# A two-layer decoder trunk in split fp32: chain steps of the token mixers grouped, at least 3.5 planner units apart

## The chip, the cores and the metric

The kernel runs on one core of one Trainium2 chip. The metric is the device time of one execution in microseconds, as the median of several runs. Besides, one execution is recorded by the hardware profiler; its trace is what the text reads.

## The reference

256 tokens of width 1024 go through two layers. Each layer is a half-step SwiGLU FFN, a token mixer, and another half-step FFN. Beside the mixer's own heads stand four heads that attend to 256 memory rows; both share one input projection and one output projection. Cut to what matters:

```python
mem_kv = rms_norm(mem, mem_norm_g) @ mem_w_kv            # keys and values of the memory heads
for i in range(2):
    x = x + 0.5 * swiglu(rms_norm(x, ffn1_norm_g[i]), ffn1_w_in[i], ffn1_w_out[i])
    hn = rms_norm(x, mix_norm_g[i])
    if i == 0:                                           # mixer A
        proj = hn @ a_w_in[0]
        y_tok = mlstm_heads(...)                         # 4 heads: decay-weighted scores, numerators, per-head norm, gate
        w_out = a_w_out[0]
    else:                                                # mixer B
        proj = hn @ b_w_in[0]
        y_tok = swa_heads(...)                           # 16 query heads, 2 key heads, window 128, sinks, QK norm, rotary
        w_out = b_w_out[0]
    y_mem = memory_heads(...)                            # QK norm, softmax over 256 rows
    x = x + concatenate([y_tok, y_mem]) @ w_out
    x = x + 0.5 * swiglu(rms_norm(x, ffn2_norm_g[i]), ffn2_w_in[i], ffn2_w_out[i])
```

## The kernel before

**Projections.** All big products are computed in three matmuls: weights and activations are split into a high part rounded to fp32r and the remainder (`split`, L211 on ScalarE for the high part, L212 on VectorE for the low part), and `mm3` (L225 to L227) multiplies high by high, high by low and low by high into one PSUM bank. A weight tile is 128x1024 and feeds 24 such matmuls. Five raw tiles and eight split pairs rotate, so loading and splitting run ahead of TensorE. This sequence of projection matmuls is called the stream here.

**Chains.** What the mixers compute between the projections are chains of small dependent steps. A step has some TensorE instructions (fp32 matmuls, or transposes through the identity, L236), and then work on VectorE, ScalarE and GpSimd whose result the chain's next step needs on TensorE. In mixer B:
- keys: one turn (`turn`, four 128x128 transposes into one bank), a scaled copy;
- each of four query groups: `head_norm` (square on ScalarE, sum L374, scale L377, a power on GpSimd L379, scale L381, product L383, which is the last reader of the group's PSUM bank), rotary embedding (L857 to L860), then a turn and a scaled copy, which spawns two `head` chains;
- `head`, for a pair of query heads: mask and scores into two banks (L920, L925), maxima (L929, L930), minima with the sink (L932, L933), exponentials (L132 is the line of every ScalarE activation), sum, reciprocal, scaling (L946); then six transposes and copies (L954); then the value product (L961) and its split (L245, L246);
- each of the two memory query groups: `head_norm`, a turn, and two memory heads: scores against `kT` (L231), maxima L591, exponentials, scaling L596; four transposes and a copy (L603); a product with `vM` (L231) and its split (L245, L246).

Mixer A has the same memory heads, and for its own four heads gate columns, scores, numerators and a turn.

**The order.** TensorE's and SyncE's instructions are issued in exactly the order in which the program emits them. The other engines' order is set by a scheduler that knows the data dependences. A planner, `Weave`, fixes TensorE's order: `run` walks the main generator (the stream), which yields after every 12 matmuls or so. `now` is the planner's own clock: every emitted matmul adds its assumed cost (0.328 for the three of `mm3`, 0.107 for a transpose). A chain yields the spacing after which its next step is due (table `LAT`, in the same units, about microseconds). After each yield of the stream all due chain steps are emitted; since a step itself moves `now`, further steps can become due in the same loop. `need` makes the stream wait for a chain's result; then the earliest step is emitted at once.

**PSUM.** There is one pool of eight banks (`mo`). Every group of projections, turn, score or product takes one; a head pair's scores take two. A new user waits for the last reader of the bank that it is given.

Of the kernel before, what the change touches and what calls it, by code (L numbers as in the profile page):

```python
# [32 lines left out]
def constants():  # L33
# [16 lines left out]

LAT = dict(pieces=1, norm=7.5, norm_b=4.8, mnorm=2.4, x0=16.0, x0_b=7.5, mkeys=7.2, cross=9.5, cross_s=1.5,
           cross_m=3.7, cross_p=8.7, cross_o=3.0, gates=20.0, scores=2.2, scores_m=8.4, num=6.9, num_r=7.5,
           keys=5.5, keys_d=7.2, query=9.0, head=1.5, head_m=2.5, head_p=9.3, head_o=4.0)


WARM = 18
# [2 lines left out]
class Weave:  # L61
# [5 lines left out]

    def __init__(self):
        self.now, self.live, self.seq = 0.0, [], 0

    def spawn(self, chain, delay=0.0):
        self.live.append([self.now + delay, self.seq, chain])
        self.seq += 1
# [12 lines left out]
    def run(self, main):  # L86
        for need in main:
            while need is not None and not need():
                self.step(min(self.live, key=lambda c: (c[0], c[1])))
            c = self.ready()  # L90
            while c is not None:
                self.step(c)
                c = self.ready()
        while self.live:
            self.step(min(self.live, key=lambda c: (c[0], c[1])))

# [2 lines left out]
def tile_trunk(ctx: ExitStack, tc: tile.TileContext, a, out):  # L99
# [11 lines left out]
    wv = Weave()  # L111
# [24 lines left out]
    def table(name):  # L136

        with tc.issue_after(tabled[0].ins):
            nc.scalar.preload_act_table_set(name)

    def unit(dt):
        return mk(up, [P, 2, T], dt, "u")

    def tmp():
        return mk(tp, [P, 2, T], F32, "t")
# [4 lines left out]
    def mo():  # L150
        return mk(pb8, [P, 512], F32, "bank")

    def halves(ps):
        return ps.rearrange("p (h t) -> p h t", h=2)
# [48 lines left out]
    pieces = [1]  # L203
# [12 lines left out]
    def wtile(src, nk, ncol=256):  # L216
        raw = mk(wrp, [P, nk, ncol], F32, "wr")
        nc.sync.dma_start(raw, src)
        return split(raw, [P, nk, ncol])
# [4 lines left out]
    def mm3(ps, wh, wl, xh, xl, start, stop):  # L224
        nc.tensor.matmul(ps, wh, xh, start=start, stop=False, skip_group_check=True)  # L225
        nc.tensor.matmul(ps, wh, xl, start=False, stop=False, skip_group_check=True)  # L226
        nc.tensor.matmul(ps, wl, xh, start=False, stop=stop, skip_group_check=True)  # L227
        wv.now += 0.328
# [28 lines left out]
    def pair(x):  # L257
        return x.unsqueeze(1).to_broadcast([P, 2, T])


    class Norm:
# [30 lines left out]

        def chain(self, gap=LAT['norm_b']):
            pc = mo()
            for h in range(2):
                mmf(pc[:, h:h + 1], self.acc[:, 0, h * P:(h + 1) * P], ones, 1)
            self.rc = mk(sp, [P, 2], F32, "rc")
            rsqrt_cols(self.rc, pc[:, 0:2], 2, 1.0 / D)
            if not self.rows:
                self.done = True  # L300
                return
            yield gap
            ps = mo()
            bcast_rows(ps, self.rc)
            self.rb = mk(sp, [P, T], F32, "rb")
            nc.scalar.copy(self.rb, ps[:, :T])
            if self.half:
                self.hrb = mk(sp, [P, T], F32, "hrb")
                act(self.hrb, ps[:, :T], AF.Copy, scale=0.5)
            self.done = True  # L310
# [57 lines left out]
    def head_norm(dst, src, n, hsc):  # L368

        hd = src.shape[2] // n  # L370
        sq, v, u = tmp(), col(), col()
        sqv = sq[:, :, :n * hd]
        act(sqv, src, AF.Square)
        nc.vector.tensor_reduce(out=v[:, 0:2 * n].rearrange("p (h m) -> p h m", h=2),  # L374
                                in_=sqv.rearrange("p h (m d) -> p h m d", m=n), axis=AX.X, op=ALU.add)
        for h in range(2):
            nc.vector.tensor_scalar(u[:, n * h:n * h + n], v[:, n * h:n * h + n], hsc[:, h:h + 1], EPS,  # L377
                                    op0=ALU.mult, op1=ALU.add)
        nc.gpsimd.tensor_tensor(out=u[:, 8:8 + 2 * n], in0=u[:, 0:2 * n], in1=mhalf[:, 0:2 * n], op=ALU.pow)  # L379
        for h in range(2):  # L380
            nc.vector.tensor_scalar(v[:, 8 + n * h:8 + n * h + n], u[:, 8 + n * h:8 + n * h + n],  # L381
                                    hsc[:, 2 + h:3 + h], None, op0=ALU.mult)
        tt(out=dst.rearrange("p h (m d) -> p h m d", m=n), in0=src.rearrange("p h (m d) -> p h m d", m=n),  # L383
           in1=v[:, 8:8 + 2 * n].rearrange("p (h m) -> p h m", h=2).unsqueeze(3).to_broadcast([P, 2, n, hd]),
           op=ALU.mult)
# [12 lines left out]
    x0 = Norm(G_F1)  # L398

    def memory():  # L400
# [22 lines left out]
        def keys(gi, kr):  # L423
            nc.scalar.copy(kT[gi], turn(kr))
            return
            yield

        for gi in range(2):
# [13 lines left out]
            norm.fold()  # L442
            wv.spawn(norm.chain(), LAT['mnorm'])
            gv = Group(wkv, 512, mh, ml, rows=True)
# [5 lines left out]
            for i, q in enumerate((first, gr)):  # L450
                kr = tmp()
                head_norm(kr, q.ps, 2, hsc)
                wv.spawn(keys(i, kr), LAT['mkeys'] + 1.5 * i)
        for gi in range(2):
# [7 lines left out]
            if gi == 0:  # L462
                with tc.issue_after(last[0].ins):
                    for c2 in range(4):
                        x0.put(xT[c2])
                wv.spawn(x0.chain(LAT['x0_b']), LAT['x0'])

# [41 lines left out]
    def ffn(x, w_in, w_out, nxt=None, mid=None):  # L509

        pieces[0] = 1
        hh, hl = [], []
        yield from ffn_in(x, w_in, hh, hl, mid)
        w = w_out.rearrange("(k p) f -> p k f", p=P)

        def products(ps, m, kg, wt, start):
            ms = slice(m * P, (m + 1) * P)
            for k in range(kg[1]):
                kc = kg[0] + k
                mm3(ps, wt[0][:, k, ms], wt[1][:, k, ms], hh[kc // 2][:, kc % 2], hl[kc // 2][:, kc % 2],  # L520
                    start=kc == 0 and start, stop=kc == 21)

        for c2 in range(4):
            wts = [(kg, w[:, kg[0]:kg[0] + kg[1], c2 * 256:(c2 + 1) * 256]) for kg in KG]
            if nxt is None and c2 == 3:
                wts = [(kg, wtile(src, kg[1])) for kg, src in wts]
                y = tmp()
                for m in range(2):
                    ps = mo()[:, :T]
                    for kg, wt in wts:  # L530
                        products(ps, m, kg, wt, True)
                        yield
                    tt(out=y[:, m], in0=ps, in1=x.hrb, op=ALU.mult)
                    tt(out=y[:, m], in0=y[:, m], in1=x.xT[c2][:, m], op=ALU.add)
                    nc.scalar.dma_start(out[:, 2 * c2 + m], y[:, m])
                return
            ps = mo()
            for kg, src in wts:
                wt = wtile(src, kg[1])
                for m in range(2):  # L540
                    products(ps[:, m * T:(m + 1) * T], m, kg, wt, m == 0)
                    yield
            t = tmp()
            tt(out=t, in0=halves(ps), in1=pair(x.hrb), op=ALU.mult)
            xn = unit(F32)
            tt(out=xn, in0=t, in1=x.xT[c2], op=ALU.add)
            if nxt is None:
                nc.scalar.dma_start(out[:, 2 * c2:2 * c2 + 2], xn)
            else:
                nxt.put(xn)  # L550
        wv.spawn(nxt.chain(), LAT['norm'])

# [15 lines left out]
    def cross_spawn(gr, gi, layer, hsc, ys):  # L568
# [4 lines left out]
        def queries():  # L573
# [4 lines left out]
            for m in range(2):  # L578
                wv.spawn(head(m), LAT['cross_s'] + LAT['cross_m'] * m)
            return  # L580
# [68 lines left out]
    def mixer_a(x, nxt):  # L649
        w = a["a_w_in"][0]  # L650
        table("sigmoid_and_others")
        pieces[0] = LAT['pieces']
        ys = Heads()
        og, qk, sd = [], {}, {}

# [207 lines left out]
    def mixer_b(x, nxt):  # L863
        w = a["b_w_in"][0]
        pieces[0] = LAT['pieces']
        table("natural_log_exp_and_others")
        ys = Heads()
        st = {}
# [107 lines left out]
    def program():  # L976
        yield from memory()
        x1, x2, x3 = Norm(G_MIX, half=False), Norm(G_F2), Norm(G_F1 + 8)
        x4, x5 = Norm(G_MIX + 8, rows=False), Norm(G_F2 + 8)
        yield from ffn(x0, a["ffn1_w_in"][0], a["ffn1_w_out"][0], x1, late_constants)  # L980
        yield from mixer_a(x1, x2)
        yield from ffn(x2, a["ffn2_w_in"][0], a["ffn2_w_out"][0], x3)
        yield from ffn(x3, a["ffn1_w_in"][1], a["ffn1_w_out"][1], x4, rope_tables)
        yield from mixer_b(x4, x5)
        yield from ffn(x5, a["ffn2_w_in"][1], a["ffn2_w_out"][1])
# [41 lines left out]
```

## Time and profile before

| | |
|---|---|
| median of three runs | 1012.15 us (1011.66 to 1013.83) |
| the profiled execution | 1012.23 us, span 1010.4 us |
| busy: TensorE, VectorE, ScalarE, GpSimd | 998.5, 655.5, 519.5, 35.7 us |
| mixer A, from its first chain step to the next norm | 257.79 to 357.75 us |
| mixer B, between the norms before and behind it | 719.40 to 833.89 us |

Times inside the trace count from the span's start. A row of the chain or of the timeline names the line of the program, the engine, the operation and the tiles written and read. TensorE's matmuls are pipelined: a row's duration contains the way through the array, so what an instruction costs is the distance from its start to the next start. A transposed or fp32 matmul is emitted once and can show as more than one instruction.

### The profile page before, as it was taken

The page shows a single profiled execution, that of the slowest core. Times are in us where ns is not written, and L with a number is a line of the kernel's source. Part 1 is how long each engine was busy: PE and PEld are TensorE (multiplying, and loading weights), DVE is VectorE, ACT ScalarE, POOL GpSimd, SP SyncE. Part 2 cuts the span into 40 slices and gives each one's busy share as a digit, 9 for nine tenths or more (in the row PEclk, how much of TensorE's full clock was granted, in tenths as well). Part 3 has the DMA queues.
Part 4 walks back from the last instruction along what each step waited for, and adds up shares of the span by engine and source line. Part 5 has one row for each costly group of instructions (what it writes and reads, how often), then busy time and mean ns, then how long its engine had stood idle before and what let it go on. Part 6 is the DMA issues. An engine that isn't in the chain of part 4 may idle for free.

```text
span 1010.4 us, 20624 instructions
## 1 busy us (share of the span) xinstructions
PE 998.5 (99%) x8594; PEld 980.2 (97%) x8594; DVE 655.5 (65%) x1063; ACT 519.5 (51%) x764; POOL 35.7 (4%) x32
## 2 busy tenths in 40 slices
PE   8999999999999999999999999999999999999998
PEld 7999999999999999999999999999987899999998
DVE  6866665577856676665558666656787766666551
ACT  7754445446656554444445544544557754454440
POOL 1200000000001000000000000000121000000000
PEclk9999999999999999999999999999999999999999
DMA  9776656666644566665676666567541347666550
GB/s 308 242 245 200 192 180 185 199 183 179 184 139 133 167 210 195 200 189 170 192 206 205 189 191 201 173 197 198 182 131 66 100 131 220 198 189 185 188 170 21
DMA packets 173204, 182.70 MB, mean 181 GB/s; under 512 B 7124, under 2 KB 168328, under 8 KB 173112
## 3 DMA queue, kind: packets, MB, share of 16 engines
q1 hardware_dynamic: 171872, 179.60, 58.3%
q10 hardware_dynamic: 1016, 1.58, 0.5%
q8 instruction: 67, 1.10, 0.5%
q0 software_dynamic: 224, 0.22, 0.2%
q14 instruction: 25, 0.20, 0.1%
HBM read 180.32 MB, written 1.05 MB: 180 GB/s over the span
## 4 chain that ended last, share of the span: by engine, by line
PE 94%; DVE 3%; ACT 1%; DMA 1%; POOL 0%; issue 0%; SPq 0%; ACTq 0%
PE bank L225 30%; PE bank L226 30%; PE bank L227 30%; PE bank L231 2%; PE bank L236 1%; ACT u L132 1%; DVE wl L212 1%; DMA wr<-in_mem_w_kv_dram 1%; PE bank L961 1%; POOL col L379 0%; DVE col L930 0%; DVE u L383 0%; DVE col L591 0%; PE bank L925 0%; DVE u L946 0%
## 5 line engine op out<-in xcount | busy, mean ns | idle before, releaser
L212 DVE TENSOR_TENSOR wl<-wr,wh 128x1024 fp32r<-128x1024 f32 (+1 forms) x347 | 414.7, 1196 | 279.8 <-ACT wh L211 279.0
L211 ACT CAST wh<-wr 128x1024 fp32r<-128x1024 f32 (+1 forms) x347 | 356.8, 1031 | 393.1 <-PE bank L226 368.9
L225 PE MATMUL bank<-xh,wh 128*128 128x256 f32 x1544 | 429.1, 278 | 0.0
L226 PE MATMUL bank<-xl,wh 128*128 128x256 f32 x1544 | 426.8, 276 | 0.0
L227 PE MATMUL bank<-xh,wl 128*128 128x256 f32 x1544 | 426.8, 276 | 0.0
L226 PEld LDWEIGHTS bank<-xl,wh 128*128 128x128 f32 x1544 | 290.3, 188 | 0.1
L225 PEld LDWEIGHTS bank<-xh,wh 128*128 128x128 f32 x1544 | 290.0, 188 | 0.1
L227 PEld LDWEIGHTS bank<-xh,wl 128*128 128x128 f32 x1544 | 289.9, 188 | 0.0
L225 PE MATMUL bank<-u,wh 128*128 128x256 f32 x896 | 249.3, 278 | 0.0
L226 PE MATMUL bank<-u,wh 128*128 128x256 f32 x896 | 247.6, 276 | 0.0
L227 PE MATMUL bank<-u,wl 128*128 128x256 f32 x896 | 247.6, 276 | 0.0
L225 PEld LDWEIGHTS bank<-u,wh 128*128 128x128 f32 x896 | 168.2, 188 | 1.9 <-issue 1.7
L226 PEld LDWEIGHTS bank<-u,wh 128*128 128x128 f32 x896 | 168.4, 188 | 0.1
L227 PEld LDWEIGHTS bank<-u,wl 128*128 128x128 f32 x896 | 168.3, 188 | 0.0
L225 PE MATMUL bank<-wh,xh 128*128 128x256 f32 x208 | 59.7, 287 | 0.0
L226 PE MATMUL bank<-wl,xh 128*128 128x256 f32 x208 | 57.9, 278 | 0.0
L227 PE MATMUL bank<-wh,xl 128*128 128x256 f32 x208 | 57.9, 278 | 0.0
L476 DVE TENSOR_TENSOR t<-bank,rb 128x256 f32<-128x256 f32 x88 | 36.6, 420 | 7.3 <-PE bank L227 7.3
L225 PEld LDWEIGHTS bank<-wh,xh 128*128 128x128 f32 x208 | 39.1, 188 | 0.5 <-issue 0.3
L226 PEld LDWEIGHTS bank<-wl,xh 128*128 128x128 f32 x208 | 39.1, 188 | 0.1
L227 PEld LDWEIGHTS bank<-wh,xl 128*128 128x128 f32 x208 | 39.0, 187 | 0.0
L479 DVE TENSOR_TENSOR t<-t,bank 128x256 f32<-128x256 f32 x88 | 32.7, 412 | 1.8 <-ACT t L132 1.8
(171 smaller groups left out, 657.5 us busy)
## 6 DMA issues: line engine op xcount, KB each, us to landing
wr<-in_ffn_w_in_dram SPq DMA_DIRECT2D x176, 512.0 KB, 3.6
wr<-in_ffn_w_out_dram SPq DMA_DIRECT2D x80, 512.0 KB, 3.5
wr<-in_a_w_in_dram SPq DMA_DIRECT2D x28, 512.0 KB, 3.9
wr<-in_b_w_in_dram SPq DMA_DIRECT2D x14, 512.0 KB, 4.6
wr<-in_a_w_out_dram SPq DMA_DIRECT2D x12, 512.0 KB, 3.3
wr<-in_b_w_out_dram SPq DMA_DIRECT2D x12, 512.0 KB, 3.4
wr<-in_ffn_w_out_dram SPq DMA_DIRECT2D x16, 256.0 KB, 2.8
wr<-in_mem_w_kv_dram SPq DMA_DIRECT2D x7, 512.0 KB, 8.0
```

Of the source, the lines that this page charges most:

```text
L132: ins = nc.scalar.activation(*args, **kw)
L211: last[0] = nc.scalar.copy(hi[:, i * n:(i + 1) * n], src[:, i * n:(i + 1) * n])
L212: tt(out=lo[:, i * n:(i + 1) * n], in0=src[:, i * n:(i + 1) * n], in1=hi[:, i * n:(i + 1) * n].bitcast(F32), op=ALU.subtract)
L225: nc.tensor.matmul(ps, wh, xh, start=start, stop=False, skip_group_check=True)
L226: nc.tensor.matmul(ps, wh, xl, start=False, stop=False, skip_group_check=True)
L227: nc.tensor.matmul(ps, wl, xh, start=False, stop=stop, skip_group_check=True)
L231: nc.tensor.matmul(ps, lhsT, rhs, start=start, stop=stop, skip_group_check=True)
L236: nc.tensor.transpose(ps, src, ident[:k, :k])
L476: tt(out=t[:, m], in0=ps[m][:, :T], in1=x.rb, op=ALU.mult)
L479: tt(out=t[:, m], in0=t[:, m], in1=ps[m][:, T:], op=ALU.mult)
L961: nc.tensor.matmul(o[es[e], cs], vr[:, i, js], pTs[e][:, src], start=i == 0, stop=i == 1, skip_group_check=True)
```

## The change

Three things. `Weave` gets a grain: after chain steps have been emitted, the next ones are emitted only when the planner's clock has moved on by `grain` units, and then all that are due. The mixers set it to 3.5, the FFNs to 0. And five spacings in `LAT` change: the memory heads' scores come 2.5 instead of 1.5 units behind their turn, the second head of a group 3.0 instead of 3.7 behind the first, the memory heads' value product 3.5 instead of 3.0 behind its copy; in mixer B the first pair's scores come 2.5 instead of 1.5 units behind the query turn, and the second pair's 1.0 instead of 2.5 behind the first.

```diff
-LAT = dict(pieces=1, norm=7.5, norm_b=4.8, mnorm=2.4, x0=16.0, x0_b=7.5, mkeys=7.2, cross=9.5, cross_s=1.5,
-           cross_m=3.7, cross_p=8.7, cross_o=3.0, gates=20.0, scores=2.2, scores_m=8.4, num=6.9, num_r=7.5,
-           keys=5.5, keys_d=7.2, query=9.0, head=1.5, head_m=2.5, head_p=9.3, head_o=4.0)
+LAT = dict(pieces=1, norm=7.5, norm_b=4.8, mnorm=2.4, x0=16.0, x0_b=7.5, mkeys=7.2, cross=9.5, cross_s=2.5,
+           cross_m=3.0, cross_p=8.7, cross_o=3.5, gates=20.0, scores=2.2, scores_m=8.4, num=6.9, num_r=7.5,
+           keys=5.5, keys_d=7.2, query=9.0, head=2.5, head_m=1.0, grain=3.5, head_p=9.3, head_o=4.0)
...
     def __init__(self):
         self.now, self.live, self.seq = 0.0, [], 0
+        self.grain, self.fired = 0.0, 0.0
...
         for need in main:
             while need is not None and not need():
                 self.step(min(self.live, key=lambda c: (c[0], c[1])))
-            c = self.ready()
+            c = self.ready() if self.now >= self.fired + self.grain else None
             while c is not None:
                 self.step(c)
                 c = self.ready()
+                self.fired = self.now
...
     def ffn(x, w_in, w_out, nxt=None, mid=None):
 
         pieces[0] = 1
+        wv.grain = 0.0
...
         pieces[0] = LAT['pieces']
+        wv.grain = LAT['grain']
```

The last pair of lines stands at the head of both mixers. No instruction is added or taken away; TensorE's order changes within the two mixers, and with it the order of the other engines there and the banks that are given out.

1 line of the change is left out of this document (added).

## The prediction

> **What bounds the kernel now.** I read the head of the page, then the windows by stage, then TensorE's waits in the second mixer, then the order of time there.
>
> ```profile
> span 1010.4 us, 20624 instructions
> ## 1 busy us (share of the span) xinstructions
> PE 998.5 (99%) x8594; PEld 980.2 (97%) x8594; DVE 655.5 (65%) x1063; ACT 519.5 (51%) x764; POOL 35.7 (4%) x32
> ```
>
> TensorE sets the time. The profiled execution took 1012.23 us, 1.83 us more than its span and 0.08 us over the median; my sum is made against 1012.23.
>
> ```profile
> 257.79:357.75 99.96, 99.96 (x814) 97.95 (x813) 67.85 (x131) 59.86 (x112) 3.21 (x4) 1.00 0.48 148
> 357.75:719.40 361.65, 361.65 (x3191) 361.65 (x3189) 230.88 (x318) 176.29 (x212) 2.24 (x2) 1.00 0.64 195
> 719.40:833.89 114.49, 109.16 (x894) 98.27 (x894) 84.99 (x233) 71.23 (x175) 13.82 (x8) 1.00 0.36 113
> ```
>
> The columns are stretch, length, then busy time (and instructions) of PE, PEld, DVE, ACT, POOL, then the granted clock. The first row is mixer A from its first chain step on, the second nearly all FFN, the third mixer B. Only the mixers' order changes, so only rows one and three can move. FFN matmuls follow each other every 361.65 / 3191 = 0.113 us. In mixer A TensorE never idles; in mixer B it idles 114.49 - 109.16 = 5.3 us:
>
> ```profile
> PE bank L231 <- ACT u L132: 1.5, 1, 1.5
> PE bank L925 <- ACT u L132: 1.4, 1, 1.4
> PE bank L231 <- ACT t L603: 1.1, 1, 1.1
> ```
>
> These and three shorter ones are chain steps whose operand was late. A matmul counts as busy for 0.28 us but its successor could have started 0.11 us after it, so each of the six waits costs about 0.17 to 0.28 us more than its row; from start to start I count **7.0 us of waits in mixer B now**.
>
> **What a switch from the stream to a chain step costs.** This is what setting steps together could save.
>
> ```profile
> 729.38 0.60 PE L236 MATMUL bank<-con,u 128*128 128x128 f32 x4
> 729.74 0.37 PE L225 MATMUL bank<-wh,xh 128*128 128x256 f32 x1
> 729.94 0.28 PE L226 MATMUL bank<-wl,xh 128*128 128x256 f32 x1
> ...
> 732.65 0.27 PE L236 MATMUL bank<-con,u 128*128 128x128 f32 x1
> ```
>
> Four transposes alone hold TensorE for 0.36 us, and the first stream matmul behind them takes 0.20 instead of 0.12. So the return costs 0.09 us. Between 729.94 and 732.65 lie 23 matmuls, one every 0.118 us: after a switch the stream runs either at 0.118 or at the FFN's 0.113, and about half of the mixers' stretches show the slow one.
>
> ```profile
> 746.27 1.04 PE L236 MATMUL bank<-con,u 128*128 128x128 f32 x8
> 747.15 1.03 PE L231 MATMUL bank<-kT,u 128*128 128x256 f32 x4
> 747.82 0.47 PE L225 MATMUL bank<-wh,xh 128*128 128x256 f32 x1
> ```
>
> Joined, two turns take 0.88 us, 0.44 each, where one alone with its return takes 0.36 + 0.09 = 0.45. A score step of a memory head takes 0.67 here. So a step set behind another pays nearly the return it saves; joining is worth 0 to 0.1 us each.
>
> **The sum, mixer A.** In the built order of the changed kernel the 17 places where chain steps interrupt mixer A's stream become 13. The links of every chain lie 36 or more stream matmuls apart (36 x 0.113 = 4.1 us), no step is brought close behind its producer, and the present trace shows no wait there. Joining saves up to 0.2 us. The cadence of 696 matmuls can turn out all fast or all slow; that is -1.3 to +1.7 us, and I take -0.2, the half and half of now.
>
> **The sum, mixer B.** 22 interruptions become 11; I take 11 x 0.1 = 1.1 us off. But the order does more than space the steps. Every step moves the planner's clock on, which makes further steps due, and the inner loop takes them all before it looks at the grain again. At the fourth interruption after the first (144 matmuls on) one bunch holds six turns (T), six of the eight head pairs' scores (H), the four value products of the memory heads and two pairs' six transposes, with no projection between. Unhindered its length is:
>
> ```profile
> 784.56 0.50 PE L920 MATMUL bank<-maskb,identb 128*128 128x384 bf16 x2
> 784.99 0.93 PE L925 MATMUL bank<-u,u 64*128 64x128 f32 x8
> 785.85 0.39 PE L225 MATMUL bank<-u,wh 128*128 128x256 f32 x1
> ```
>
> H is 785.85 - 784.56 = 1.29 us; 6 x 1.29 + 6 x 0.44 + 4 x 0.67 (value products as the score step) + 2 x 0.66 (six transposes as 6/8 of 0.88) = 14.4 us. It starts at about 751.0: 729.38, plus four stretches of 36 with their return (4.3 to 4.4 each), plus steps of 0.36, 0.36, 1.1 and 2.5 us.
>
> Does what it needs exist by then? The first limit is the vector queue, which is worked off strictly in order.
>
> ```profile
> 736.10 0.68 DVE L374 TENSOR_REDUCE col<-t 128x8 f32<-128x512 f32 x1
> 736.82 0.36 DVE L377 TENSOR_SCALAR col<-col,qsc 128x4 f32<-128x4 f32 x2
> 737.09 1.22 DVE L212 TENSOR_TENSOR wl<-wr,wh 128x1024 fp32r<-128x1024 f32 x1
> 739.84 0.36 DVE L381 TENSOR_SCALAR col<-col,qsc 128x4 f32<-128x4 f32 x2 [1.53 <-POOL col L379]
> 740.11 0.68 DVE L591 TENSOR_REDUCE col<-bank 128x2 f32<-128x512 f32 x1
> 740.71 0.68 DVE L383 TENSOR_TENSOR u<-bank,col 128x512 f32<-128x512 f32 x1
> ```
>
> ```profile
> L212 DVE TENSOR_TENSOR wl<-wr,wh 128x1024 fp32r<-128x1024 f32 x26 | 31.5, 1220 | 10.6 <-ACT wh L211 10.6
> ...
> L383 DVE TENSOR_TENSOR u<-bank,col 128x512 f32<-128x512 f32 x6 | 4.1, 688 | 0.3
> ...
> L596 DVE TENSOR_TENSOR u<-u,col 128x512 f32<-128x512 f32 x4 | 2.7, 687 | 0.1
> L591 DVE TENSOR_REDUCE col<-bank 128x2 f32<-128x512 f32 x4 | 2.7, 681 | 0.0
> ```
>
> ```profile
> L379 POOL TENSOR_TENSOR col<-col,mhalf 128x8 f32<-128x8 f32 x4 | 8.3, 2073 | 38.6 <-DVE col L377 38.6
> ```
>
> A query group's norm is L374, L377, a power on POOL, L381, L383. Up to the first group's L374 the queues stand as before, so 736.10 holds. From there to the third group's L383 the changed vector order has five weight subtractions (6.1), three L374 and three L383 (4.1), maxima and scalings of four memory heads (4 x 0.681 + 4 x 0.687 = 5.5), and small ones: twelve L377/L381 at 0.18 (2.2), two ropes (estimated 2), reciprocals (0.6). That is 20.5 us, less 2.5 because a successor starts some 0.07 us before its forerunner's end. In two of the three norms L381 now stands right behind L377, where L212 stood between: the queue idles a whole power (2.07 each), in the third most of it is covered (0.9 left). Waits for exponentials add an estimated 1.3. So the third L383 ends at 736.1 + 20.5 - 2.5 + 5.0 + 1.3 = 760.4. TensorE wants the PSUM bank which it frees for the bunch's fourth turn, at 751.0 + 3 x 0.44 + 2 x 1.29 = 754.9, and loses **5.5 us** there or just before. At present projections stand between these parts.
>
> The second limit is ScalarE. The first pair's maxima stand behind that L383, so its exponentials begin at about 762.8.
>
> ```profile
> 756.68 0.37 ACT L132 ACTIVATE u<-bank,col 128x128 f32<-128x128 f32 x1 [2.02 <-DVE col L932]
> ...
> 758.37 0.38 ACT L132 ACTIVATE u<-bank,col 128x128 f32<-128x128 f32 x1
> ```
>
> ```profile
> L954 ACT COPY t<-bank 128x384 f32<-128x384 f32 x16 | 7.0, 493 | 1.2 <-PE bank L236 1.0
> L132 ACT ACTIVATE u<-bank,col 128x128 f32<-128x128 f32 x16 | 6.0, 376 | 10.3 <-DVE col L932 10.3
> L245 ACT CAST u<-bank 128x256 fp32r<-128x256 f32 x12 | 4.6, 386 | 4.1 <-PE bank L961 3.9
> L132 ACT ACTIVATE t<-bank 128x512 f32<-128x512 f32 x6 | 3.7, 616 | 2.3 <-PE bank L227 2.3
> ```
>
> One pair takes 758.37 - 756.68 = 1.69 us. The bunch's last scores need a bank that the fourth pair's second exponential frees: three pairs (5.1), four L245, two L954, three copies of 512 (4.4), two exponentials (0.8), with some 1.6 us of waits for maxima, so 762.8 + 11.9 = 774.7; scores then end at 775.8. The bunch lasts 24.8 instead of 14.4 us: **10.4 us of waits**. Two interruptions later the fourth group's L383 stands behind four L954 and another power; its bank and one behind it, freed by an L246 that a rope and an L212 precede, are late by an estimated 1 + 2 us. The remaining steps lie far enough apart. Waits in mixer B: 13.4 against 7.0. Sum: 1012.2 + 6.4 - 1.1 - 0.2 = **1017.3 us**. POOL's power took from 1.0 to 2.5 us in single cases, and what stands between the powers is estimated; +-3 us on the waits and the cadence give 1013.9 to 1021.5 for this case.
>
> DMA is no term: the projections' weight tiles are prefetched eight deep, and SP's order of transfers is the same.
>
> The granted clock is 1.00 in all three rows above, with waits of up to 1.5 us. [...]
>
> **The rivals.** *Faster, the vector queue in time.* Each microsecond by which the third L383 ends ahead of 760.4 takes one off. If the powers take 1.0 us and nothing waits for exponentials, and the queue's small items are half of mine, it ends near 754 (760.4 - 3.0 - 1.3 - 2.4); the bunch then ends near 769 with 3.7 us of waits, and if the fourth group's 3 us shrink to 1 likewise, mixer B has 4.7 instead of 7.0: 1012.2 - 2.3 - 1.3 = 1008.6. It decides at about 755: a later end makes the kernel slower. For it: DVE is busy only 85 of 114 us in mixer B. Against it: its idle time lies mostly at the end, where no chain is left.
>
> *No change, cadence and joining.* 1320 matmuls of the mixers run half at 0.118. If the longer stretches all came out at 0.113, that is 2.9 us off; with 3 us less of waits than I count the time is 1017.3 - 2.9 - 3 = 1011.4, and 1009 to 1014 with either alone or more. For it: stretches behind some turns return to 0.113 at once. Against it: nothing in the order selects them.
>
> [...]
>
> **How the numbers follow.** The forecast has 0.62, the vector queue in time 0.16, cadence and joining 0.18 (0.12 within 0.2%, about what a measurement of this kernel can tell, and 0.06 faster), the clock 0.04. Slower by over 0.2% (above 1014.2): 0.66; within: 0.12; faster: 0.22. The range reaches from 1008.0, which leaves out about a tenth below, to 1021.5.
>
> **What would show it.** Right: one interruption of some 25 us in mixer B, about 22 us after its first turn, with waits for L383 and for exponentials; mixer B near 120 us, mixer A within 1.5 us of 99.96, the other stretches unchanged. Wrong: a bunch under 18 us, or mixer A off by over 2 us. The joining is wrong if two turns and a score step together cost over 0.3 us less than apart.

## The result, and the profile after

| | before | after |
|---|---|---|
| median of 18 runs each | 1012.35 us (1011.66 to 1013.88) | 1015.13 us (1014.30 to 1017.24) |
| profiled execution: time, span | 1012.23, 1010.4 us | 1015.03, 1013.2 us |
| ratio after to before | | 1.0024, 95% interval 1.0017 to 1.0032 |

The changed kernel is slower. The direction was forecast, the size was not: the medians differ by 2.8 us where 5.1 were forecast. By the ratio and its interval, the loss is 0.17 to 0.32%, or 1.7 to 3.2 us.

The head of the page of the changed kernel shows the same instructions on TensorE and the same busy time; the span is 2.8 us longer.

```profile
span 1013.2 us, 20631 instructions
PE 998.6 (99%) x8594; PEld 981.3 (97%) x8594; DVE 655.2 (65%) x1063; ACT 519.3 (51%) x764; POOL 32.4 (3%) x32
```

The windows by stage, cut at the same events as before (mixer A from its first chain step, the FFNs, mixer B):

```profile
257.93:357.83 99.90, 99.90 (x815) 98.00 (x814) 67.82 (x131) 59.79 (x112) 2.79 (x4) 1.00 0.47 148
357.83:719.47 361.64, 361.64 (x3190) 361.64 (x3189) 230.89 (x318) 176.31 (x212) 2.24 (x2) 1.00 0.64 195
719.47:836.75 117.28, 110.10 (x894) 99.58 (x894) 85.08 (x233) 70.95 (x175) 12.99 (x8) 0.97 0.35 110
```

Mixer A has 99.90 us (99.96 before), the FFNs 361.64 (361.65). All of the difference lies in mixer B: 117.28 against 114.49 us. Its granted clock is 0.97, not 1.00; that comes from one place, the bunch.

The bunch in the order of time on TensorE, where the number in brackets is the idle time ahead of a row and what ended it (at the second row that is a reciprocal, L598, the last event that the trace shows there):

```profile
751.63 0.60 PE L238 MATMUL bank<-con,u 128*128 128x128 f32 x4
752.64 0.63 PE L238 MATMUL bank<-con,u 128*128 128x128 f32 x4 [0.41 <-DVE col L598]
...
756.75 0.32 PE L925 MATMUL bank<-maskb,identb 128*128 128x384 bf16 x1 [1.55 <-ACT u L134]
...
761.08 1.12 PE L238 MATMUL bank<-con,u 128*128 128x128 f32 x4 [3.16 <-DVE u L385]
761.99 1.92 PE L233 MATMUL bank<-t,vM 128*128 128x256 f32 x4
763.70 1.06 PE L238 MATMUL bank<-con,u 128*128 128x128 f32 x4
...
768.45 1.03 PE L233 MATMUL bank<-t,vM 128*128 128x256 f32 x4
769.31 0.49 PE L925 MATMUL bank<-maskb,identb 128*128 128x384 bf16 x2
...
771.70 0.48 PE L925 MATMUL bank<-maskb,identb 128*128 128x384 bf16 x2 [0.24 <-ACT t L959]
...
774.75 0.32 PE L925 MATMUL bank<-maskb,identb 128*128 128x384 bf16 x1 [0.56 <-ACT u L134]
...
775.86 0.39 PE L227 MATMUL bank<-wh,xh 128*128 128x256 f32 x1
```

It begins at 751.63 and the stream returns at 775.86: 24.23 us for one interruption. The turn at 761.08 waits for the product of the third query group's norm (L383 before, L385 here). The vector queue ahead of it:

```profile
755.68 0.67 DVE L376 TENSOR_REDUCE col<-t 128x8 f32<-128x512 f32 x1
...
756.86 0.35 DVE L379 TENSOR_SCALAR col<-col,qsc 128x4 f32<-128x4 f32 x2
757.13 1.22 DVE L214 TENSOR_TENSOR wl<-wr,wh 128x1024 fp32r<-128x1024 f32 x1
759.87 0.36 DVE L383 TENSOR_SCALAR col<-col,qsc 128x4 f32<-128x4 f32 x2 [1.53 <-POOL col L381]
760.34 0.69 DVE L385 TENSOR_TENSOR u<-bank,col 128x512 f32<-128x512 f32 x1
760.95 0.28 DVE L934 TENSOR_REDUCE col<-bank 128x1 f32<-128x128 f32 x1
```

The product ends at 761.03, and the turn starts 0.05 us later. The first pair's maxima (L934) stand right behind the product, though that pair's scores were done at about 754.4; its exponentials follow only then, on ScalarE:

```profile
762.99 0.37 ACT L134 ACTIVATE u<-bank,col 128x128 f32<-128x128 f32 x1 [5.34 <-DVE col L937]
...
764.69 0.38 ACT L134 ACTIVATE u<-bank,col 128x128 f32<-128x128 f32 x1
```

What the forecast's sum did not have is the granted clock (the third column from the end) in four windows of the bunch:

```profile
757.00:761.08 4.08, 0.92 (x9) 0.52 (x8) 2.45 (x7) 0.66 (x2) 2.54 (x1) 0.67 0.59 203
761.08:764.55 3.47, 3.47 (x12) 2.95 (x13) 3.33 (x16) 1.56 (x8) 0.00 (x0) 0.50 0.03 8
764.55:766.18 1.63, 1.63 (x12) 0.68 (x10) 1.33 (x7) 1.63 (x10) 0.00 (x0) 0.79 0.00 0
766.18:768.01 1.83, 1.83 (x11) 1.49 (x9) 1.81 (x10) 1.83 (x7) 0.00 (x0) 1.00 0.00 0
```

A mean of 0.67 over 4.08 us is half speed in its last 2.7 us; 0.79 over 1.63 us is half speed in its first 0.7. So the clock was halved from 758.4 to 765.2, 6.8 us. The product at 761.99 holds TensorE for 1.71 us (to 763.70), where one of the same shape takes 0.86 later on (768.45 to 769.31).

The next interruption, and the one after it, the fourth query group's place:

```profile
780.29 1.52 PE L966 MATMUL bank<-t,u 128*64 128x256 f32 x16
781.74 1.53 PE L238 MATMUL bank<-con,u 128*128 128x128 f32 x12
783.03 0.37 PE L227 MATMUL bank<-u,wh 128*128 128x256 f32 x1
...
787.30 1.52 PE L966 MATMUL bank<-t,u 128*64 128x256 f32 x16
788.75 0.87 PE L238 MATMUL bank<-con,u 128*128 128x128 f32 x6
790.78 0.87 PE L238 MATMUL bank<-con,u 128*128 128x128 f32 x6 [1.16 <-DVE u L248]
791.41 0.36 PE L227 MATMUL bank<-u,wh 128*128 128x256 f32 x1
```

The latter takes 4.11 us, where 28 instructions of the same kinds took 2.74 at 780.29: one wait, for L248, and none for the product L385.

### The profile page after: what moved, and what is told of

It reads as the page before. It is cut to its first block, busy times and chain, and to the rows that moved or that the text cites. A ratio compares the mean times of both kernels' runs of the same rounds, so it can differ in the third digit from the quotient of the medians.

```text
span 1013.2 us, 20631 instructions
## 1 busy us (share of the span) xinstructions
PE 998.6 (99%) x8594; PEld 981.3 (97%) x8594; DVE 655.2 (65%) x1063; ACT 519.3 (51%) x764; POOL 32.4 (3%) x32
## 3 DMA queue, kind: packets, MB, share of 16 engines
q10 hardware_dynamic: 1016, 1.58, 0.5%
## 5 line engine op out<-in xcount | busy, mean ns | idle before, releaser
L214 DVE TENSOR_TENSOR wl<-wr,wh 128x1024 fp32r<-128x1024 f32 (+1 forms) x347 | 414.6, 1196 | 288.7 <-ACT wh L213 287.7
```

The costliest lines, as they stand in the source:

```text
L214: tt(out=lo[:, i * n:(i + 1) * n], in0=src[:, i * n:(i + 1) * n], in1=hi[:, i * n:(i + 1) * n].bitcast(F32), op=ALU.subtract)
```

## The experiments

For all of them mixer B is given from the first matmul of the norm step ahead of it to that of the norm step behind it (0.36 us more than the window that starts behind the norm step; expectations may count either way). "Bunch" is its longest interruption. An FFN stretch in which the stream ran at 0.118 us throughout costs some 6.5 us more; it is told beside mixer B, since it hides what a kernel's order does. It comes and goes between executions of one kernel (e4's runs lie at 1015 to 1016 or at 1022 to 1024 us; the one in its trace, at 1015.06, has none), so the medians mix both, and mixer B in the trace is the better measure of the order. Some executions also have a low clock early on: in the traces of e10, e11 and e12 the mean over the whole execution is 0.997 or 0.998, with 1.00 in the windows from 40 to 1004 us, and mixer B begins at 720.61 to 720.66 us, against 719.04 to 719.26 before, after and in e4 and e9. Mixer B has a spread of its own: each kernel has one trace, and kernels whose order in mixer B is the same on every engine gave 118.31 and 117.49 us (e1, e4) and 115.33 and 114.53 (e10, e13 below), since more of the stream ran at 0.118 in the longer ones (474 matmuls against 281, 478 against 288). So differences under 0.8 us in that column are not told apart.

| kernel | grain | spacings | mixer B | bunch | slow FFN stretch in the trace | median, us | ratio to before |
|---|---|---|---|---|---|---|---|
| before | none | old | 114.86 | 6.98 | none | 1012.35 | 1 |
| after | both mixers | new | 117.64 | 24.23 | none | 1015.13 | 1.0024 [1.0017, 1.0032] |
| e1 | mixer A | new | 118.31 | 7.52 | last | 1022.69 | 1.0082 [1.0054, 1.0110] |
| e2 | both, only steps due at entry | new | 123.16 | 11.79 | none | 1020.23 | 1.0067 [1.0046, 1.0088] |
| e3 | none, two steps at a time | new | 123.69 | 9.92 | none | 1021.92 | 1.0082 [1.0059, 1.0105] |
| e7 | none, one step at a time | new | 121.41 | 6.06 | last | 1020.21 | 1.0070 [1.0053, 1.0086] |
| e4 | none | new | 117.49 | 7.53 | none | 1022.04 | 1.0070 [1.0044, 1.0095] |
| e8 | both mixers | old | 118.49 | 19.11 | none | 1016.90 | 1.0042 [1.0030, 1.0054] |
| e9 | none | new for memory heads | 115.97 | 7.51 | none | 1013.45 | 1.0005 [0.9994, 1.0016] |
| e10 | none | new for query heads | 115.33 | 6.98 | last | 1019.80 | 1.0081 [1.0064, 1.0099] |
| e5 | after, no power | new | 109.77 | 18.18 | first | 1013.42 | 0.9993 [0.9971, 1.0015] |
| e6 | before, no power | old | 110.25 | 6.67 | first | 1013.85 | 0.9987 [0.9963, 1.0011] |
| e11 | after, power on ScalarE | new | 109.69 | 18.14 | none | 1008.18 | 0.9960 [0.9948, 0.9972] |
| e12 | before, power on ScalarE | old | 110.37 | 6.79 | none | 1007.84 | 0.9958 [0.9945, 0.9972] |

**Is it the bunch? e1: the grain in mixer A alone.** In mixer B:

```diff
-        wv.grain = LAT['grain']
+        wv.grain = 0.0
```

> The changed kernel with the grain in mixer A alone; the new spacings stay in both mixers. Theory bunch (the loss is the waits of the one long bunch in mixer B, which only the grain builds): mixer A stays at 99.9 us, mixer B has no group of chain steps over 10 us and lies within 1.5 us of the 114.5 of before; time 1011 to 1013.5. Rival spacings (the longer spacings themselves delay the chains): mixer B stays near 117.3 and the time near 1015.

Measured: without the bunch mixer B is no shorter, 118.31 us, as the rival said. The stream is broken 22 times again, and its longest interruptions take 6.6, 7.5, 6.1 and 5.7 us. So taking away the bunch does not give back the loss: the smaller orders that the new spacings make have waits of their own.

**e2: only the steps due at entry.** The inner loop no longer takes what its own steps make due.

```diff
-            c = self.ready() if self.now >= self.fired + self.grain else None
-            while c is not None:
+            due = [c for c in self.live if c[0] <= self.now] if self.now >= self.fired + self.grain else []
+            for c in sorted(due, key=lambda c: c[1]):
                 self.step(c)
-                c = self.ready()
+            if due:
                 self.fired = self.now
```

> The changed kernel, but the inner loop emits only the steps that were due when it was entered; what becomes due while it runs waits for the next grain. Mixer B's largest group is then five turns' worth of transposes, two products and three pairs of scores instead of 112 instructions of every kind. Theory bunch: mixer B loses most of the 9.8 us of waits of the bunch and lasts 108 to 113 us, time 1006 to 1011, so faster than both. Rival grain (spacing steps 3.5 units apart delays the chains whatever the groups): 1014 to 1017.

Measured: mixer B 123.16 us, far outside both expectations. The bunch is halved and the chains end later. Here the clock halves under the stream itself:

```profile
768.79:774.45 5.66, 5.66 (x25) 5.37 (x26) 3.83 (x7) 2.94 (x5) 2.40 (x1) 0.50 0.31 97
```

24 stream matmuls take 5.66 us, 0.236 each on the mean; at a clock of 1.00 they take 0.113 or 0.118.

**e3 and e7: two steps, and one step, after each yield.** Without grain:

```diff
-            c = self.ready() if self.now >= self.fired + self.grain else None
-            while c is not None:
+            c, n = (self.ready() if self.now >= self.fired + self.grain else None), 0
+            while c is not None and n < 2:
                 self.step(c)
-                c = self.ready()
+                c, n = self.ready(), n + 1
```

> The new spacings, no grain, but at most two chain steps after each yield of the stream, in both mixers: no group of steps in mixer B holds more than a few. Theory bunch: waits in mixer B fall below the 7 us of before, mixer B 109 to 113 us, while mixer A has 19 interruptions instead of 17 and stays within 1 us of 99.96; time 1007 to 1011. Rival (few interruptions are what counts): mixer B has more interruptions than in either kernel and gets longer than 114.5, time 1013 to 1016.

> The new spacings, no grain, and one chain step at most after each yield of the stream: mixer A has 26 interruptions instead of 17 (before) and 13 (changed), none with a wait near, so mixer A alone prices an interruption. Theory (a step set behind another pays nearly the return it saves): mixer A 99.96 plus 0 to 0.1 us each, so 100 to 101, give or take 1.5 for the stream's two cadences. Rival (each interruption costs a fixed 0.3 us or more): mixer A 103 or longer. Mixer B: waits fall, but its last steps come 60 matmuls later; 109 to 114 us. Time 1007 to 1013.

Measured: mixer B 123.69 and 121.41 us, where 109 to 113 and 109 to 114 were expected: smaller groups do not take the waits away. e7 also prices the interruption as such: mixer A took 133.81 us with 27 interruptions, 133.95 with the 18 of before (the 17 of the prediction and the one behind its norm step) and 133.89 with the 14 of after, from norm to norm. Interrupting the stream costs nothing that can be seen there. (e3's mixer A, with 20, took 134.72; one wait of 0.3 us is in it.)

**e4 and e8: the spacings alone, and the grain alone.** e4 sets the grain to 0 in both mixers, e8 keeps the grain and takes back the five spacings:

```diff
-           ... head=2.5, head_m=1.0, grain=3.5, head_p=9.3, head_o=4.0)
+           ... head=2.5, head_m=1.0, grain=0.0, head_p=9.3, head_o=4.0)
```

> The new spacings without any grain (the order in mixer B is that of e1). Theory bunch: mixer B as in e1 within 0.5 us, mixer A with 17 interruptions within 1 us of 99.96, time 1011 to 1013.5. Rival spacings: mixer B near 117, time near 1015. Beside e1 it prices the grain in mixer A alone: joining worth 0.2 us there, so the two differ by less than 1 us.

> The grain of 3.5 in both mixers with the five spacings of before; it completes the square with the changed kernel (both) and the spacings alone (mixer B 117.49). Its biggest bunch is smaller by two turns, two pairs' scores and one value product than the changed kernel's. Theory 'spacings' (the five longer or shorter spacings alone put steps where operands are late, and the grain on top costs nothing): mixer B 113.5 to 115.5, as before. Theory 'bunch' (the grain's one big interruption costs by itself, and the spacings cost by another way that the grain removes): mixer B 116.5 to 119. Mixer A 133.9 from norm to norm by both.

Measured: mixer B grows by 2.6 us with the spacings alone, by 3.6 with the grain alone, and by 2.8 with both. Each part costs by itself about what both cost together, so the two costs don't add. e8's 118.49 lies in the range of its theory 'bunch', in which the two parts cost by different ways. The rows of the waits speak for one and the same limit, products of the vector queue that come late; they don't prove it, for the power was not taken out of these two kernels. In e4, in small pieces:

```profile
753.10 0.63 PE L238 MATMUL bank<-con,u 128*128 128x128 f32 x4 [0.95 <-DVE u L385]
...
783.41 0.32 PE L925 MATMUL bank<-maskb,identb 128*128 128x384 bf16 x1 [1.25 <-DVE u L385]
```

and in e8 in one piece, for one product of that line:

```profile
762.03 0.82 PE L925 MATMUL bank<-maskb,identb 128*128 128x384 bf16 x2 [3.10 <-DVE u L385]
```

In e8 the clock is halved as well, from 757.6 to 767.8 us. By the distances of the same steps at full clock the work under it is some 3.4 us longer (an estimate), so how e8's loss divides between the waits and the clock stays open. e4's clock is 1.00 all through mixer B.

**e9 and e10: the spacings in two halves.** Without grain, e9 changes the three of the memory heads, e10 the two of the query heads.

> No grain; only the three spacings of the memory heads are changed (2.5, 3.0, 3.5), the two of the query heads are those of before. TensorE's order up to the sixth interruption behind the memory scores is the same as with all five spacings. If the memory heads' spacings carry the loss of the spacings alone: mixer B 116.5 to 118. If the query heads' do: 114 to 115.

> No grain; only the two spacings of the query heads' scores are changed (2.5, 1.0), the three of the memory heads are those of before. If the memory heads' spacings carry the loss of the spacings alone: mixer B 114 to 115. If the query heads' do: 116.5 to 118.

Measured: 115.97 and 115.33 us, +1.1 and +0.5; both expected that one half would carry the loss, and neither does. The +0.5 is within the spread (e13, with the same order in mixer B, took 114.53). Together they cost 2.6, so an interplay of 1 us or more is left that no run splits further. e10 is also a warning: its mixer B is 0.5 us longer than before, its median 7.5. The window of its last FFN stretch, and that of the changed kernel:

```profile
842.30:1014.64 172.34, 172.34 (x1465) 172.34 (x1465) 93.20 (x119) 69.00 (x80) 0.00 (x0) 1.00 0.49 159
```

```profile
843.24:1009.12 165.88, 165.88 (x1466) 165.88 (x1465) 93.22 (x119) 69.08 (x80) 0.00 (x0) 1.00 0.54 165
```

The same matmuls, TensorE never idle, the clock 1.00, and 6.5 us apart.

**e5 and e6: the power taken out.** In both kernels GpSimd's power in the norm is replaced by a VectorE instruction that writes 1.0, so that the inverse root is left out of the norms of queries, keys and memory queries in both mixers:

```diff
-        nc.gpsimd.tensor_tensor(out=u[:, 8:8 + 2 * n], in0=u[:, 0:2 * n], in1=mhalf[:, 0:2 * n], op=ALU.pow)
+        nc.vector.tensor_scalar(u[:, 8:8 + 2 * n], u[:, 0:2 * n], 0.0, 1.0, op0=ALU.mult, op1=ALU.add)
```

> The changed kernel with GpSimd's power in the query and key norms replaced by a small VectorE instruction that writes 1.0 (so the inverse root is left out of these norms). The order of the projections and chain steps on TensorE is the same. Theory of the two limits (the bunch waits first for the vector queue, which idles behind the power, then for ScalarE): the L383 of the third query group ends some 5 us earlier, the bunch shrinks from 24.2 to 18.5 to 20.5 us, the 4.1 us group behind it to about 2.9; time 1009 to 1011.5. Rival (ScalarE's work alone sets the bunch): the bunch stays above 22 us, time above 1013.

> The same replacement in the kernel before. Theory: three of the six waits there follow a norm, so mixer B gains 2 to 4 us: 1008.5 to 1010.5; after e5 the change would then cost 0 to 2 us instead of 2.8. Rival (the power is covered in the finer order): under 1 us of gain, above 1011.5.

Measured: the changed kernel's bunch falls from 24.23 to 18.18 us, the fourth group's interruption from 4.11 to 2.92, mixer B to 109.77. The kernel before comes to 110.25. Both traces have a slow first FFN stretch, which hides the gain in the medians. Without the power the change costs nothing in mixer B; it is 0.5 us shorter there, which is within the spread.

**e11 and e12: the power on ScalarE.** The same with the values kept, in mixer B's norms:

```diff
-        nc.gpsimd.tensor_tensor(out=u[:, 8:8 + 2 * n], in0=u[:, 0:2 * n], in1=mhalf[:, 0:2 * n], op=ALU.pow)
+        if lnexp[0]:
+            act(u[:, 8:8 + 2 * n], u[:, 0:2 * n], AF.Ln)
+            act(u[:, 8:8 + 2 * n], u[:, 8:8 + 2 * n], AF.Exp, scale=-0.5)
+        else:
+            nc.gpsimd.tensor_tensor(out=u[:, 8:8 + 2 * n], in0=u[:, 0:2 * n], in1=mhalf[:, 0:2 * n], op=ALU.pow)
...
+        lnexp[0] = True
```

> The changed kernel, with the power on GpSimd in mixer B's norms of queries and memory queries replaced by a logarithm and an exponential of -0.5 times it on ScalarE (same values). Theory 'two limits' (the vector queue idles behind the power, then ScalarE's exponentials end the bunch): the power of 1.0 to 2.5 us becomes two small activations, some 0.5 us with their start, so the bunch falls from 24.2 to 18.5 to 21 us and mixer B from 117.3 to 110.5 to 113.5. Rival: the two activations queue on ScalarE behind weight casts of 1.2 us and copies, so nothing is won: bunch 23 to 26 us, mixer B 116.5 to 119.

> The kernel before with the same replacement as in the run of the changed kernel with logarithm and exponential on ScalarE (mixer B 109.69 there, 117.64 without it, from norm to norm). Theory 'the change costs through the vector queue behind the power': with the short norm the kernel before gains less, since its finer order hid more of the power; mixer B 109.5 to 111.5 (from 114.86), so that the two orders come out within 1 us of each other. Rival 'the change costs by its order itself': the kernel before gains as much as the changed one (8 us): mixer B 106.5 to 108.

Measured: mixer B 109.69 and 110.37 us; medians of 1008.18 and 1007.84 us, both faster than the kernel before by about 4 us and not to be told from each other. Mixer B of the changed kernel lies a little below its expectation. Its third query group's norm, on VectorE and on ScalarE:

```profile
754.11 0.35 DVE L381 TENSOR_SCALAR col<-col,qsc 128x4 f32<-128x4 f32 x2
754.37 1.22 DVE L214 TENSOR_TENSOR wl<-wr,wh 128x1024 fp32r<-128x1024 f32 x1
755.50 0.35 DVE L389 TENSOR_SCALAR col<-col,qsc 128x4 f32<-128x4 f32 x2
...
755.97 0.68 DVE L391 TENSOR_TENSOR u<-bank,col 128x512 f32<-128x512 f32 x1
```

```profile
754.50 0.45 ACT L134 ACTIVATE col<-col 128x8 f32<-128x8 f32 x2 [0.69 <-DVE col L381]
...
758.41 0.37 ACT L134 ACTIVATE u<-bank,col 128x128 f32<-128x128 f32 x1 [1.87 <-DVE col L944]
```

Logarithm and exponential take 0.45 us together and are done within the weight subtraction (L214), so VectorE's queue doesn't idle. The first pair's exponentials start 5.3 us into the bunch (753.12 here) instead of 11.4, and the bunch is 6.1 us shorter. This shows the prediction's first limit.

**e13 and e14: what sets the cadence.** Four lone 128x128 transposes, read by nothing, are set into the last FFN, in e10's kernel (whose last stretch was slow) and in the changed one (whose was fast):

```diff
+    def poke():
+        transpose(mo()[:, :P], ident)
...
         for gi in range(11):
+            if lastffn[0] and gi in (3, 7):
+                poke()
...
         for c2 in range(4):
+            if lastffn[0] and c2 in (0, 2):
+                poke()
```

> The kernel with only the query heads' spacings changed, whose last FFN stretch of 1464 matmuls ran at 117.8 ns each (1018.5 to 1025 us), with four lone 128x128 transposes set into the last FFN (behind its third and seventh group of columns and ahead of the first and third quarter of its output). Nothing reads what they write. Theory 'drawn anew at every return': the five parts of the stretch run each at 113.3 or 117.8 ns, not all at 117.8, and the median falls by 2 to 6 us, to 1013 to 1017. Rival 'fixed by the kernel or by the data stretch': all five parts at 117.8, 1019 to 1020.5.

> The changed kernel, whose last FFN stretch ran at 113.3 ns per matmul throughout, with the same four lone transposes (each 0.1 us and up to 0.1 us for the return, 0.4 to 0.8 us together). Theory 'drawn anew at every return': one or more of the parts behind a transpose can run at 117.8 ns, 1015.5 to 1021 us. Rival 'fixed by the kernel': all parts at 113.3, 1015 to 1016.

Measured: 1016.7 and 1018.8 us, both in the ranges of 'drawn anew'. In both traces the five parts run fast, slow, fast, fast, slow. (e14's span is 1016.7 us, the changed kernel's 1013.2.) Two of e13's parts, 384 matmuls each:

```profile
861.12:906.43 45.31, 45.31 (x388) 45.31 (x386) 27.70 (x36) 20.98 (x24) 0.00 (x0) 1.00 0.58 186
906.45:950.09 43.64, 43.64 (x388) 43.64 (x387) 27.16 (x36) 20.61 (x24) 0.00 (x0) 1.00 0.58 188
```

0.118 and 0.114 us each, with one transpose between them. So the cadence changed here where the stream returned from a single transpose, and then held; e10's slow stretch became partly fast in e13, and the changed kernel's fast one partly slow in e14. That both kernels show the same five parts says that it isn't plain chance; what decides it stays open.

**e15 and e16: TensorE kept busy in the long wait.** In the changed kernel 24, and 8, transposes of the identity into the unused columns of a score bank, right ahead of the turn that waits 3.16 us:

```diff
+        heads = []
...
+            heads.append(ch)
+            if len(heads) == 2:
+                for _ in range(24):
+                    nc.tensor.transpose(sc[1][:, 384:], ident, ident)
```

> The changed kernel with 24 transposes of the identity (about 0.09 us each, 2.2 us) into the unused columns 384 to 511 of a score bank, right ahead of the bunch's turn that waits 3.16 us for the third query group's norm; they fit into that wait and nothing reads them. Theory 'the halved clock costs' : TensorE stays busy, the granted clock stays at 1.00, the 4.2 us of work behind the wait take 2.1 us less, the bunch falls from 24.2 to 22.0 to 22.8 us, mixer B from 117.6 (norm to norm) to 115.3 to 116.3. Rival 'ScalarE's exponentials would hold the bunch anyway': the clock stays at 1.00 and the bunch at 23.8 to 24.4, with new waits for exponentials of about 2 us behind 762. Third: the clock falls all the same (the share of busy time ahead of the wait decides), nothing changes.

> The same with 8 transposes, 0.7 us of the 3.16 us wait filled, so that 2.4 us of idle time are left behind them. If a single idle stretch of about 3 us is what halves the clock, it stays at 1.00 and the bunch is as with 24. If the share of busy time over some 3 to 4 us decides, it falls to 0.50 all the same, and the bunch stays near 24.2 us.

Measured: medians of 1017.24 and 1015.73 us. With 8 the clock stays at 1.00 through the bunch, and the bunch takes 24.82 us. In place of the lost clock TensorE waits for ScalarE:

```profile
753.22:778.04 24.82, 18.11 (x122) 11.54 (x120) 20.58 (x76) 16.79 (x66) 2.54 (x1) 1.00 0.12 43
```

```profile
762.68 0.66 PE L238 MATMUL bank<-con,u 128*128 128x128 f32 x4 [2.14 <-DVE u L385]
...
765.55 0.32 PE L927 MATMUL bank<-maskb,identb 128*128 128x384 bf16 x1 [0.91 <-ACT u L134]
766.36 0.32 PE L927 MATMUL bank<-maskb,identb 128*128 128x384 bf16 x1 [0.48 <-ACT u L134]
```

With 24 the bunch takes 26.51 us: the clock is 1.00 up to 765.42 and halves behind it, after the same two waits (0.92 and 0.48 us there).

```profile
765.42:769.32 3.90, 3.52 (x11) 2.31 (x10) 2.26 (x11) 2.75 (x12) 0.00 (x0) 0.56 0.00 0
```

This fits none of the three cases told ahead of e15. e16, whose clock stays up, bears out the rival in the main (its range for the bunch ended at 24.4): ScalarE's exponentials, queued behind the late product, hold TensorE about as long as the halved clock did. The scores behind these two waits start 3.93 us behind the turn in e16 (766.61) and 4.24 in the changed kernel (765.32), so the halved clock cost at most 0.3 us up to there. Further on the two can't be compared, for VectorE's order differs from about there on. Nor was the halved clock free in every run. e14, with the changed kernel's order in mixer B on every engine and the same wait of 3.16 us, has the low clock 1.5 us later, so that it covers 1.5 us more of the work:

```profile
759.91:766.74 6.83, 5.65 (x22) 4.03 (x22) 5.81 (x25) 3.75 (x19) 0.00 (x0) 0.50 0.16 61
```

Its bunch takes 24.91 us, 0.7 more than the changed kernel's. So where the low stretch falls is worth up to some 1 us (0.3 + 0.7, an estimate). The loss of 2.8 us does not need the clock: e4 loses 2.6 with the clock at 1.00.

## Why the prediction was right, and where it was wrong

Right: the direction, the place and the mechanism. One interruption of 24.23 us (24.8 forecast) begins at 751.63 (751.0); mixer A and the FFNs stay; the third query group's product ends at 761.03 (760.4). Up to the turn behind it TensorE works 3.9 us by the prediction's rows and 9.45 pass: 5.5 us of waits, as forecast. e5 and e11 confirm the first limit (the power), e16 the second (the exponentials).

Some of that fit is luck. The vector queue's idle time behind the three powers came to 5.03 us against 5.0, but in parts it was 1.75, 1.75 and 1.53 against 2.07, 2.07 and 0.9: the two powers that stand uncovered took 1.64 us each, and the third 2.54.

Wrong: the sum of mixer B, +5.3 forecast and +2.8 measured. Two terms failed by their size, the waits in the bunch and those at the fourth group. The measured column takes each distance from start to start on TensorE in mixer B less the usual distance of the same pair of instructions at clock 1.00 in these traces. The row of returns and cadence is what is left of the measured difference; the last point below finds the same 0.9 another way.

| term of mixer B | forecast | measured |
|---|---|---|
| waits in the bunch (measured: with 2.1 of halved clock) | 10.4 | 8.9 |
| waits at the fourth group | 3 | 1.3 |
| waits now, taken off | -7.0 | -6.5 |
| fewer returns, cadence | -1.1 | -0.9 |
| sum | +5.3 | +2.8 |

- **The fourth group's 1 + 2 us** is the term that failed most: 1.7 too much. It was not worked out from rows but estimated. L385 was in time for its bank, and only the wait for L248 came (1.16 us in its row).
- **The bunch's 10.4** is 1.5 too much. The bunch was 0.6 shorter than forecast, and some 0.9 of what was counted as wait is work. The prediction priced a value product at 0.67, as a score step ahead of the stream. In the bunch, with another step behind it, it takes 0.86 (768.45 to 769.31), and there are four: that is 0.8 of the 0.9. Behind the turn at 761.08, 14.78 us pass with 11.4 of work: 3.4 are lost where 4.9 were forecast. 2.1 of the 3.4 are the halved clock's, under the steps up to 766.18, and 1.3 are waits.
- **The present waits** were counted 0.5 too high, which made the forecast loss smaller and hid part of the error: from start to start the six rows and one short wait of 0.16 us come to 6.5.
- **Joining.** The 624 stream matmuls of mixer B and the changes around them take 77.51 us before and 74.42 after. Of these 3.1 us, 2.15 are two waits that stood ahead of a step before (1.61 and 0.54 over the cadence) and that the prediction had among its 7.0. The other 0.9 are the joining: 46 intervals around switches became 24, at 0.067 us each over the cadence (-1.4), less 434 slow matmuls instead of 316 (+0.5). The forecast's 1.1 came near since a gain and a loss that it left out nearly cancel.

**The rivals.** *The vector queue in time* did not come: the product ended at 761.0, not near 754. e11 shows what short powers give: a bunch of 18.1 us, and no loss against e12. *Cadence and joining*: both were small here, but the cadence was priced far too low. The forecast let it act on the mixers' 1320 matmuls, for 2.9 us at most; it also takes hold of an FFN stretch of some 1464 matmuls and is worth 6.5 us there. *The clock*, which had a chance of 0.04, did halve: from 758.4 to 765.2 us, beginning 0.5 us into the wait of 3.16 us. The rows of before have a clock of 1.00 and show nothing that would lower it, so the chance was the author's guess. What ran under the low clock was the bunch's own steps, and most of it was covered by the exponentials (0.3 us at most up to the third pair's scores). In e7 the clock halved behind gaps of 1.59 and 2.03 us; it was low for 6.8 us here and for 3.4 there.

**And a premise.** The prediction took the bunch for the cause of the loss. e1 and e4 contradict it: without the bunch the new spacings lose as much. In the changed kernel the limit is the vector queue, idle behind GpSimd's power while TensorE waits for a product or a bank. That the other orders with all five new spacings press on the same limit is read from their waits for VectorE, and was not tested by itself; with the power gone from that queue the orders of before and after come out within 1 us of each other (e5 and e6, e11 and e12).

## What to carry to other kernels

When steps of dependent chains are moved or joined, first find the in-order queue that feeds them all, and price the idle time in it that the present order covers; a shorter operation there (here 0.45 us for a power of 2.07 on the mean) was worth 4 us of the whole, where none of the regroupings of steps gained. Work out each wait from rows, the small ones behind the main one too, price each step with the neighbour that it will have, and take off the present waits with the same care: the difference is small against both. And where medians of kernels with the same stages differ by several us, compare the stages that were not touched before the edit is blamed.

## What the runs showed of the hardware that was not expected

**Two cadences.** The stream of 128x256 fp32r matmuls runs at 113.3 or 117.8 ns per matmul, with TensorE always busy and the clock at 1.00 in both. It changed at a single transpose in e13 (0.118 us each up to 906.43, 0.114 behind it), and without other steps it held through the FFN stretches of before and after, up to 1536 matmuls in a row at 113.3. In an FFN stretch of 1464 it is worth 6.5 us (172.34 in e10, 165.88 after), more than the whole change.

**The clock.** In e7 it halved at 769.20, behind two scores' waits of 1.59 and 2.03 us with 0.3 us of work between them, and stayed low for 3.40 us:

```profile
766.02 0.32 PE L925 MATMUL bank<-maskb,identb 128*128 128x384 bf16 x1 [1.59 <-DVE u L248]
768.38 0.34 PE L925 MATMUL bank<-maskb,identb 128*128 128x384 bf16 x1 [2.03 <-DVE u L385]
```

```profile
769.20:772.60 3.40, 3.40 (x16) 1.58 (x13) 3.18 (x10) 0.67 (x3) 0.00 (x0) 0.50 0.21 52
```

In e16 the last wait of the bunch's first part was 2.14 us, longer than either of these two, and the clock stayed at 1.00. In the changed kernel and in e14 the same wait of 3.16 us had the clock fall at 758.4 and at 759.9, and it was low for 6.8 us in both. So the length of the longest single gap does not sort these cases; what decides when the clock falls was not tested.
